# Recurrence scores of a gated linear mixer: 32-frame cells in 32-column matmuls in place of three 128-wide levels

## Chip, core and metric

One core of one Trainium2 chip runs the whole kernel in a single launch. The metric is the time of the device in microseconds, and the kernel before was timed three times: 842.62, 845.66 and 846.02 us, median 845.66 us.

## What is computed

The reference is one layer of an encoder over 512 frames of 1024 channels: RMSNorm, one wide input projection, a gMLP branch, an HGRN2 gated linear recurrence of 8 heads, sigmoid merge gates, an output projection, and a squared-ReLU MLP, all in fp32. The change touches only the recurrence. For one head, with q, k, f and v of 128 channels each:

```
S_t = diag(f_t) S_{t-1} + k_t v_t^T          o_t = S_t^T q_t
# evaluated by chunks; inside a chunk
scores[t, s] = sum_d q[t, d] * k[s, d] * prod_{s < u <= t} f[u, d]     for s <= t, else 0
o_intra = scores @ v
```

The product of gates between s and t differs in every channel, so a score is a matmul only after the decays have been multiplied into the queries and the keys. The kernels do so by levels of distance between s and t.

## The kernel before, in words

A fp32 weight or activation is split into a high and a low part of a faster fp32 format (`split`, L93 to L95: ScalarE writes H, VectorE writes L), and a product is three matmuls (`mm3`, L118 to L120). Weights come in tiles of 128x1024 by DMA (`raw`, 4 buffers) and are split into `WH` and `WL` (5 buffers each).

The recurrence runs in four rounds of two heads. `proj_round` projects values V (`tok_proj`), then F, K and Q of each head (`chan_proj`), channels on partitions and the 512 frames (4 tiles of 128) on the free axis. `hgrn_head` makes the scores of one head. The tile framework orders the instructions of each engine by its own estimate of the times, so the matmuls of a head stand between projection matmuls of later rounds, or of the output gate ZO after the last one. [...]

In `hgrn_head`:

- The diagonal: q*k (L412, VectorE), split (L415, L416), two 512-wide matmuls with a matrix of ones (`dg`, L418, L419), and a predicated copy of 512 columns into `scores` (L420).
- Three levels with b = 1, 4, 16 frames in a block. Each holds the queries of 4 blocks in a group, times the decays to 6 pairs of blocks (`QX`, L436, L438), and multiplies them with all 128 keys of the tile: four matmuls of 128 columns by 192 moving columns a level (`sp`, L443). Where key and query form one of the pairs, a predicated copy takes the value into `scores` (L452, three copies for each half of the frames). Then queries and keys are moved on to the next level by more decay (L468 to L479).
- The level of 64 frames: four matmuls of 64 by 64 in half of TensorE's columns (L485), copied by ScalarE (L487), then K and Q moved on (L490 to L496).
- K turned onto frames (`pk`, L500), tile states (`pst`, L505; `st`, L507 to L511), the output (`po`, L515, L517) and its norm (L519 to L523).

Every fp32 matmul is recorded as two weight loads and two matmuls: the 96 matmuls of L443 in the program stand as 192 in the trace.

Of the kernel before, what the change touches and what calls it, by code (L numbers as in the profile page):

```python
# [8 lines left out]
F32 = mybir.dt.float32  # L9
F32R = mybir.dt.float32r  # L10
I32 = mybir.dt.int32
AF = mybir.ActivationFunctionType
ALU = mybir.AluOpType
AX = mybir.AxisListType

P = 128
S = 512
D = 1024
NT = S // P
# [11 lines left out]

RADIX = [1, 4, 16]
PAIRS = [(1, 1), (2, 1), (3, 1), (2, 2), (3, 2), (3, 3)]


# [34 lines left out]
def trunk_kernel(ctx: ExitStack, tc: tile.TileContext, A: dict, out: bass.AP):  # L72
    nc = tc.nc
# [4 lines left out]
    wp = ctx.enter_context(tc.tile_pool(name="wp", bufs=1))  # L78
# [110 lines left out]
    ident = cst.tile([P, P], F32, name="ident")  # L189
# [153 lines left out]
    for t in range(NT):  # L343
        stt6 = gp.tile([P, 6], F32, tag="bn6", bufs=2, name="bn6")
        nc.vector.bn_stats(stt6, v[:, t, :])
        mv = gp.tile([P, 2], F32, tag="mv", bufs=2, name="mv")
# [5 lines left out]
    for g in range(NG):  # L352
# [6 lines left out]
        m = gp.tile([P, NT, P], F32, tag="m", bufs=2, name="m")  # L359
# [8 lines left out]
    hg = left2.enter_context(tc.tile_pool(name="hg", bufs=1, side="left", reuse_waits="tile"))  # L368
    ps_sc = left2.enter_context(tc.tile_pool(name="ps_sc", bufs=1, space=bass.MemoryType.PSUM))
    nc.sync.dma_start(hng, A["hg_norm_g"].rearrange("o v -> v o"))  # L370
    mask = []
    for lv, b in enumerate(RADIX):
        m = hg.tile([P, 384], I32, name=f"mask{b}")
        nc.sync.dma_start(m, A[f"mask{b}"])
        mask.append(m)
    diag = hg.tile([P, P], I32, name="diag")
    nc.sync.dma_start(diag, A["diag"])
    all_ones = hg.tile([P, P], F32R, name="all_ones")
    nc.vector.tensor_scalar(all_ones, ident, 0.0, 1.0, ALU.mult, ALU.add)
    scores = [hg.tile([P, NT, P], F32, name=f"scores{i}") for i in range(2)]  # L380
    for sc in scores:
        nc.gpsimd.memset(sc, 0.0)


    def proj_round(r):
# [7 lines left out]
        for h in (2 * r, 2 * r + 1):  # L393
# [5 lines left out]
            zq = chan_proj(ZQ + 128 * h)  # L399
            Q = hg.tile([P, S], F32, tag="Q1", bufs=2, name=f"Q1_{h}")  # L400
            sq = hg.tile([P, S], F32, tag="sq", bufs=2, name=f"sq{h}")
# [4 lines left out]

    def hgrn_head(V, h, F, K, Q):
        hc = slice((h % 2) * P, (h % 2 + 1) * P)
        sc = scores[h % 2]

        qk = wp.tile([P, S], F32, tag="S", bufs=2, name=f"qk{h}")
        nc.vector.tensor_tensor(qk, Q, K, ALU.mult)  # L412
        qkH = hg.tile([P, S], F32R, tag="qkH", bufs=2, name=f"qkH{h}")
        qkL = hg.tile([P, S], F32R, tag="qkL", bufs=2, name=f"qkL{h}")
        nc.scalar.activation(qkH, qk, AF.Copy)  # L415
        nc.vector.tensor_tensor(qkL, qk, qkH.bitcast(F32), ALU.subtract)  # L416
        dg = ps_sc.tile([P, S], F32, tag="sp", bufs=4, name=f"dg{h}")
        nc.tensor.matmul(dg, all_ones, qkH, start=True, stop=False)  # L418
        nc.tensor.matmul(dg, all_ones, qkL, start=False, stop=True)  # L419
        nc.vector.copy_predicated(sc, diag[:, None, :].broadcast_to([P, NT, P]),  # L420
                                  dg.rearrange("p (t c) -> p t c", c=P))
        QX = hg.tile([P, 7 * S // 4], F32, tag="QX", bufs=4, name=f"QX1_{h}").rearrange("p (g x b) -> p g x b", x=7, b=1)
        nc.vector.tensor_tensor(QX[:, :, 0:4, 0], Q.rearrange("p (g i) -> p g i", i=4),
                                F.rearrange("p (g i) -> p g i", i=4), ALU.mult)

        T = F
        for lv, b in enumerate(RADIX):
            G, g = S // (4 * b), P // (4 * b)  # L430
            T4 = T[:, :4 * G].rearrange("p (g i) -> p g i", i=4)

            def bc(t, n=G, b=b):
                return t[:, :, None].broadcast_to([P, n, b])

            nc.vector.tensor_tensor(QX[:, :, 4:6, :], QX[:, :, 2:4, :],  # L436
                                    T4[:, :, 1:3, None].broadcast_to([P, G, 2, b]), ALU.mult)
            nc.vector.tensor_tensor(QX[:, :, 6, :], QX[:, :, 5, :], bc(T4[:, :, 1]), ALU.mult)  # L438
            for t0 in range(0, NT, 2):
                sp = ps_sc.tile([P, S], F32, tag="sp", bufs=4, name=f"sp{h}_{b}_{t0}")  # L440
                for j in range(2):
                    t = t0 + j
                    nc.tensor.matmul(  # L443
                        sp[:, j * 192:(j + 1) * 192].rearrange("p (g c) -> p g c", g=g),
                        K[:, t * P:(t + 1) * P],
                        QX[:, t * g:(t + 1) * g, 1:7, :].rearrange("p g x b -> p g (x b)"),
                        start=True, stop=True)
                spv = sp[:, :384].rearrange("p (g x b) -> p g x b", x=6, b=b)
                mv = mask[lv].rearrange("p (g x b) -> p g x b", x=6, b=b)
                scv = sc[:, t0:t0 + 2, :].rearrange("p t (g i b) -> p (t g) i b", i=4, b=b)  # L450
                for x0, n, i0 in [(0, 3, 1), (3, 2, 2), (5, 1, 3)]:
                    nc.vector.copy_predicated(scv[:, :, i0:i0 + n, :], mv[:, :, x0:x0 + n, :],  # L452
                                              spv[:, :, x0:x0 + n, :])

            b4 = 4 * b
            if b < 16:
                QN = hg.tile([P, 7 * S // 4], F32, tag="QX", bufs=4, name=f"QX{b4}_{h}").rearrange("p (g x b) -> p g x b", x=7, b=b4)
                qn = QN[:, :, 0:4, :].rearrange("p g i (j b) -> p g i j b", b=b)
                n4 = 4
            else:  # L460
                QN = hg.tile([P, S], F32, tag="Q64", bufs=2, name=f"Q64_{h}")
                qn = QN.rearrange("p (g i j b) -> p g i j b", i=1, j=4, b=b)
                n4 = 1

            def grp(x, n4=n4):
                return x.rearrange("p (g i) b -> p g i b", i=n4)

            nc.scalar.copy(qn[:, :, :, 0, :], grp(QX[:, :, 0, :]))  # L468
            for j, x in ((1, 1), (2, 4), (3, 6)):
                nc.vector.tensor_tensor(qn[:, :, :, j, :], grp(QX[:, :, x, :]), grp(bc(T4[:, :, 0])), ALU.mult)  # L470
            U = hg.tile([P, G, 2], F32, tag=f"U{b}", bufs=2, name=f"U{b}_{h}")
            Tn = hg.tile([P, G], F32, tag=f"T{b}", bufs=2, name=f"T{b}_{h}")
            nc.vector.tensor_tensor(U[:, :, 1], T4[:, :, 2], T4[:, :, 3], ALU.mult)
            nc.vector.tensor_tensor(U[:, :, 0], T4[:, :, 1], U[:, :, 1], ALU.mult)
            nc.vector.tensor_tensor(Tn, T4[:, :, 0], U[:, :, 0], ALU.mult)
            kv = K.rearrange("p (g i b) -> p g i b", i=4, b=b)
            nc.vector.tensor_tensor(kv[:, :, 0:2, :], kv[:, :, 0:2, :],
                                    U[:, :, :, None].broadcast_to([P, G, 2, b]), ALU.mult)
            nc.vector.tensor_tensor(kv[:, :, 2, :], kv[:, :, 2, :], bc(T4[:, :, 3]), ALU.mult)  # L479
            QX, T = QN, Tn  # L480

        Q = QX
        sp = ps_sc.tile([P, 512], F32, tag="sp", bufs=4, name=f"sp{h}_64")
        for t in range(NT):
            nc.tensor.matmul(sp[0:64, t * 64:(t + 1) * 64], K[:, t * P:t * P + 64],  # L485
                             Q[:, t * P + 64:(t + 1) * P], start=True, stop=True)
        nc.scalar.copy(sc[0:64, :, 64:128], sp[0:64, 0:256].rearrange("p (t c) -> p t c", c=64))  # L487
        T2 = T.rearrange("p (t i) -> p t i", i=2)
        qv = Q.rearrange("p (t i b) -> p t i b", i=2, b=64)
        kv = K.rearrange("p (t i b) -> p t i b", i=2, b=64)  # L490
        Tt = hg.tile([P, NT], F32, tag="Tt", bufs=2, name=f"Tt_{h}")
        nc.vector.tensor_tensor(kv[:, :, 0, :], kv[:, :, 0, :],
                                T2[:, :, 1:2].broadcast_to([P, NT, 64]), ALU.mult)
        nc.vector.tensor_tensor(qv[:, :, 1, :], qv[:, :, 1, :],
                                T2[:, :, 0:1].broadcast_to([P, NT, 64]), ALU.mult)
        nc.vector.tensor_tensor(Tt, T2[:, :, 0], T2[:, :, 1], ALU.mult)  # L496

        pk = ps.tile([P, NT, P], F32, tag="hm", bufs=2, name=f"pk{h}")
        for t in range(NT - 1):
# [14 lines left out]
        for t in range(NT):  # L514
            nc.tensor.matmul(po[:, t, :], sc[:, t, :], V[:, t, hc], start=True, stop=t == 0)  # L515
            if t:
                nc.tensor.matmul(po[:, t, :], Q[:, t * P:(t + 1) * P], st[:, t - 1, :],  # L517
                                 start=False, stop=True)
# [139 lines left out]
    for f in range(NPLAIN, NF, 2):  # L658
        g = acts[f // 8][:, f % 8:f % 8 + 2, :]
# [26 lines left out]
    for t in range(NT):  # L686
        for hf in range(2):
            for f in range(NSLOW - 2, NSLOW):
                ff2(f, t, hf)
            c = x2[:, t, hf * S:(hf + 1) * S]  # L690
# [151 lines left out]
def _mask(b):  # L842

    import numpy as np

    s = np.arange(P)
    m = np.zeros((P, 2, P // (4 * b), len(PAIRS), b), np.int32)
    for g in range(P // (4 * b)):
        for x, (i, d) in enumerate(PAIRS):
            m[:, :, g, x, :] = (s // b == 4 * g + i - d)[:, None, None]  # L850
    return m.reshape(P, -1)


# [35 lines left out]
```

## Time and profile before

| | us |
|---|---|
| median of three runs | 845.66 |
| the profiled execution | 845.11 |
| its span, first to last instruction | 843.3 |
| TensorE (PE) busy | 826.8 |
| VectorE (DVE) busy | 637.1 |
| ScalarE (ACT) busy | 401.7 |

The recurrence occupies TensorE, between projections, from about 98 to 283 us. PE's weight loads (PEld) are shown apart from its matmuls, and consecutive matmuls overlap in the records, so the distance from start to start is what one costs, not its own duration.

### The profile page before, as it was taken

What the parts mean: (1) busy time and instruction counts of PE and PEld (TensorE: products, weight loads), DVE (VectorE), ACT (ScalarE), POOL (GpSimd) and SP (SyncE); (2) the same over time, 40 slices, a digit from 0 to 9 for tenths busy, and PEclk for the clock granted to TensorE, in tenths of its full rate; (3) what the DMA queues carried; (4) which work ended last, traced back from release to release, by engine and by line L of the source; (5) the groups of instructions that cost most, each with busy time, mean ns of one, the idle gap of its engine ahead of it and who ended that gap; (6) DMA issues with size and microseconds to landing.
All of it is one profiled execution on the core that took longest, in us unless ns stands there. A gap on an engine that the chain in (4) does not pass through costs nothing.

```text
span 843.3 us, 13369 instructions
## 1 busy us (share of the span) xinstructions
PE 826.8 (98%) x5282; PEld 745.7 (88%) x5282; DVE 637.1 (76%) x1092; ACT 401.7 (48%) x644; POOL 47.6 (6%) x79
## 2 busy tenths in 40 slices
PE   8999999999999999999999999899999999999996
PEld 7989898989889997999978889899999988778884
DVE  6563888979799587888565349877777574899996
ACT  6433433333242345656533332777766642555464
POOL 2000000001001000000000012000000000010103
PEclk9999999999999999999999999999999999999999
DMA  9233212121221121233423412132332295193802
GB/s 334 87 117 115 100 51 75 44 83 51 75 76 51 51 76 57 74 120 108 147 103 120 167 63 96 67 109 101 119 108 101 100 293 183 27 301 85 242 17 99
DMA packets 26912, 92.68 MB, mean 110 GB/s; under 512 B 3361, under 2 KB 3873, under 8 KB 26850
## 3 DMA queue, kind: packets, MB, share of 16 engines
q1 hardware_dynamic: 24546, 84.49, 28.2%
q0 software_dynamic: 1728, 6.29, 4.2%
q10 hardware_dynamic: 576, 1.05, 0.3%
q8 instruction: 41, 0.67, 0.3%
q14 instruction: 21, 0.17, 0.1%
HBM read 89.72 MB, written 2.10 MB: 109 GB/s over the span
## 4 chain that ended last, share of the span: by engine, by line
PE 94%; ACT 2%; issue 1%; DVE 1%; DMA 1%; POOL 0%; SPq 0%; POOLq 0%; ACTq 0%; DVEq 0%
PE acc L118 14%; PE acc L119 14%; PE acc L120 14%; PE prodx L118 5%; PE prodx L120 5%; PE prodx L119 5%; PE sp L443 4%; PE prodzy L119 4%; PE prodzy L118 4%; PE prodzy L120 4%; PE hm L119 3%; PE hm L120 3%; PE hm L118 3%; PE y L119 2%; PE y L118 2%; PE y L120 2%
## 5 line engine op out<-in xcount | busy, mean ns | idle before, releaser
L95 DVE TENSOR_TENSOR WL<-raw,WH 128x1024 fp32r<-128x1024 f32 (+1 forms) x134 | 152.1, 1138 | 100.3 <-ACT WH L94 99.3
L94 ACT ACTIVATE WH<-raw 128x1024 fp32r<-128x1024 f32 (+1 forms) x134 | 132.3, 989 | 182.0 <-PE acc L119 68.3
L118 PE MATMUL acc<-WH,hTH 128*128 128x256 f32 x320 | 91.7, 287 | 0.2 <-ACT hTH L94 0.2
L120 PE MATMUL acc<-WH,hTL 128*128 128x256 f32 x320 | 91.6, 286 | 0.0
L119 PE MATMUL acc<-WL,hTH 128*128 128x256 f32 x320 | 90.6, 283 | 0.0
L120 PE MATMUL acc<-hTH,WL 128*128 128x512 f32 x160 | 64.3, 402 | 0.0
L119 PE MATMUL acc<-hTL,WH 128*128 128x512 f32 x160 | 64.1, 401 | 0.0
L118 PE MATMUL acc<-hTH,WH 128*128 128x512 f32 x160 | 64.1, 400 | 0.0
L95 DVE TENSOR_TENSOR WL<-s,WH 128x1024 fp32r<-128x1024 f32 x44 | 53.8, 1223 | 9.8 <-ACT WH L94 9.0
L118 PEld LDWEIGHTS acc<-WH,hTH 128*128 128x128 f32 x320 | 60.4, 189 | 0.4 <-ACT hTH L94 0.4
L120 PEld LDWEIGHTS acc<-WH,hTL 128*128 128x128 f32 x320 | 60.3, 189 | 0.1
L119 PEld LDWEIGHTS acc<-WL,hTH 128*128 128x128 f32 x320 | 60.3, 189 | 0.0
L94 ACT ACTIVATE WH<-s 128x1024 fp32r<-128x1024 f32 x44 | 46.7, 1062 | 14.6 <-PE prodx L119 9.5
L452 DVE COPY_PREDICATED scores<-mask,sp 128x192 f32<-128x192 int32 (+2 forms) x144 | 44.1, 360 | 6.8 <-PE sp L443 6.4
L119 PE MATMUL hm<-WL,aH 128*128 128x512 f32 x96 | 38.1, 397 | 0.0
L120 PE MATMUL hm<-WH,aL 128*128 128x512 f32 x96 | 38.0, 396 | 0.0
L118 PE MATMUL hm<-WH,aH 128*128 128x512 f32 x96 | 37.9, 396 | 0.0
L443 PE MATMUL sp<-QX,K 128*128 128x192 f32 x192 | 35.9, 326 | 0.0
L120 PEld LDWEIGHTS acc<-hTH,WL 128*128 128x128 f32 x160 | 30.1, 188 | 6.4
L119 PEld LDWEIGHTS acc<-hTL,WH 128*128 128x128 f32 x160 | 30.1, 188 | 6.4
L118 PEld LDWEIGHTS acc<-hTH,WH 128*128 128x128 f32 x160 | 30.1, 188 | 6.2
L94 ACT ACTIVATE WH<-rawx 128x1024 fp32r<-128x1024 f32 x24 | 25.1, 1053 | 18.5 <-issue 10.7
(298 smaller groups left out, 2408.2 us busy)
## 6 DMA issues: line engine op xcount, KB each, us to landing
raw<-in_w_dram SPq DMA_DIRECT2D x128, 512.0 KB, 3.5
rawx<-in_w_dram SPq DMA_DIRECT2D x18, 512.0 KB, 8.1
rawx<-in_w_dram POOLq DMA_DIRECT2D x6, 512.0 KB, 6.4
raw<-in_w_dram POOLq DMA_DIRECT2D x6, 512.0 KB, 8.0
x_t<-in_x_dram SPq DMA_DIRECT2D x4, 512.0 KB, 5.9
x<-in_x_dram SPq DMA_DIRECT2D x4, 512.0 KB, 5.6
out_dram<-x ACTq DMA_DIRECT2D x4, 256.0 KB, 2.8
out_dram<-x SPq DMA_DIRECT2D x4, 256.0 KB, 2.4
```

Source lines behind the costliest of these rows:

```text
L94: nc.scalar.activation(H, src, AF.Copy)
L95: nc.vector.tensor_tensor(L, src, H.bitcast(F32), ALU.subtract)
L118: nc.tensor.matmul(acc, ah, bh, start=first and i == 0, stop=False, **kw)
L119: nc.tensor.matmul(acc, ah, bl, start=False, stop=False, **kw)
L120: nc.tensor.matmul(acc, al, bh, start=False, stop=last and i == n - 1, **kw)
L443: nc.tensor.matmul(sp[:, j * 192:(j + 1) * 192].rearrange("p (g c) -> p g c", g=g), K[:, t * P:(t + 1) * P], QX[:, t * g:(t + 1) * g, 1:7, ...
L452: nc.vector.copy_predicated(scv[:, :, i0:i0 + n, :], mv[:, :, x0:x0 + n, :], spv[:, :, x0:x0 + n, :])
```

## The change

The scores of a tile are no longer made 128 keys wide. A tile of 128 frames is cut into four cells of 32 frames (`C = 32`, `NC = 4`). Up to blocks of 16, key and query lie in one cell, so a matmul takes 32 keys as stationary columns and the queries of the same cell only, and writes to the 32 output partitions of that cell: its own quarter of TensorE's columns. The result of a level is compact: all four tiles of a head fit in one bank, and one set of predicated copies takes it into `cells`.

- Diagonal: q times k as 16 matmuls of 32 by 32; product, split, ones matmuls and the 512-wide copy are gone.
- Levels 1 and 4: 16 matmuls of 32 keys by 48 moving columns, in place of 4 of 128 by 192. The predicated copies stand behind the updates of K and Q in the code, three a level in place of six.
- Level 16 is replaced by two halvings: blocks of 16 (16 matmuls of 32 by 16) and blocks of 32 (8 matmuls of 32 by 32), each followed by an in-place update of K and Q (`double`).
- ScalarE moves the four cells and the two 32-frame blocks into `scores` (six copies of 32 partitions).
- Level 64 is as before (L512 in the changed kernel).

```diff
-RADIX = [1, 4, 16]
+RADIX = [1, 4]
+C = 32
+NC = P // C
...
-        qk = wp.tile([P, S], F32, tag="S", bufs=2, name=f"qk{h}")
-        nc.vector.tensor_tensor(qk, Q, K, ALU.mult)
...
-        nc.scalar.activation(qkH, qk, AF.Copy)
-        nc.vector.tensor_tensor(qkL, qk, qkH.bitcast(F32), ALU.subtract)
-        dg = ps_sc.tile([P, S], F32, tag="sp", bufs=4, name=f"dg{h}")
-        nc.tensor.matmul(dg, all_ones, qkH, start=True, stop=False)
-        nc.tensor.matmul(dg, all_ones, qkL, start=False, stop=True)
-        nc.vector.copy_predicated(sc, diag[:, None, :].broadcast_to([P, NT, P]),
-                                  dg.rearrange("p (t c) -> p t c", c=P))
+        def cellwise(sp, x, n, of=1):
+            for t in range(NT):
+                for p in range(0, NC, of):
+                    nc.tensor.matmul(sp[p * C:(p + 1) * C, t * n:(t + 1) * n],
+                                     K[:, t * P + p * C:t * P + (p + 1) * C], x(t, p), start=True, stop=True)
...
+        sp = bank(0)
+        cellwise(sp, lambda t, p: Q[:, t * P + p * C:t * P + (p + 1) * C], C)
+        nc.vector.copy_predicated(cl.rearrange("p t c -> p (t c)"), mask[0], sp[:, :NT * C])
...
-            for t0 in range(0, NT, 2):
-                sp = ps_sc.tile([P, S], F32, tag="sp", bufs=4, name=f"sp{h}_{b}_{t0}")
-                for j in range(2):
-                    t = t0 + j
-                    nc.tensor.matmul(
-                        sp[:, j * 192:(j + 1) * 192].rearrange("p (g c) -> p g c", g=g),
-                        K[:, t * P:(t + 1) * P],
-                        QX[:, t * g:(t + 1) * g, 1:7, :].rearrange("p g x b -> p g (x b)"),
-                        start=True, stop=True)
...
-                for x0, n, i0 in [(0, 3, 1), (3, 2, 2), (5, 1, 3)]:
-                    nc.vector.copy_predicated(scv[:, :, i0:i0 + n, :], mv[:, :, x0:x0 + n, :],
-                                              spv[:, :, x0:x0 + n, :])
+            sp = bank(b)
+            cellwise(sp, lambda t, p: QX[:, (t * NC + p) * g:(t * NC + p + 1) * g, 1:7, :].rearrange(
+                "p g x b -> p g (x b)"), 6 * g * b)
...
+            for x0, n, i0 in [(0, 3, 1), (3, 2, 2), (5, 1, 3)]:
+                nc.vector.copy_predicated(clv[:, :, i0:i0 + n, :], mv[:, :, x0:x0 + n, :],
+                                          spv[:, :, x0:x0 + n, :])
...
+        def double(T, b):
+            n = S // (2 * b)
+            T2 = T.rearrange("p (g i) -> p g i", i=2)
+            Tn = hg.tile([P, n], F32, tag=f"T{b}", bufs=2, name=f"T{b}_{h}")
+            nc.vector.tensor_tensor(Tn, T2[:, :, 0], T2[:, :, 1], ALU.mult)
+            qv = Q.rearrange("p (g i b) -> p g i b", i=2, b=b)
+            kv = K.rearrange("p (g i b) -> p g i b", i=2, b=b)
+            nc.vector.tensor_tensor(kv[:, :, 0, :], kv[:, :, 0, :], T2[:, :, 1:2].broadcast_to([P, n, b]), ALU.mult)
+            nc.vector.tensor_tensor(qv[:, :, 1, :], qv[:, :, 1, :], T2[:, :, 0:1].broadcast_to([P, n, b]), ALU.mult)
+            return Tn
...
+        sp = bank(16)
+        cellwise(sp, lambda t, p: Q[:, t * P + p * C + 16:t * P + (p + 1) * C], 16)
+        T = double(T, 16)
+        nc.vector.copy_predicated(cl[:, :, 16:32], mask[3].rearrange("p (t c) -> p t c", t=NT),
+                                  sp[:, :NT * 16].rearrange("p (t c) -> p t c", t=NT))
+        for p in range(NC):
+            nc.scalar.copy(sc[p * C:(p + 1) * C, :, p * C:(p + 1) * C], cl[p * C:(p + 1) * C])
+        sp = bank(32)
+        cellwise(sp, lambda t, p: Q[:, t * P + (p + 1) * C:t * P + (p + 2) * C], C, 2)
+        for p in range(0, NC, 2):
+            nc.scalar.copy(sc[p * C:(p + 1) * C, :, (p + 1) * C:(p + 2) * C],
+                           sp[p * C:(p + 1) * C, :NT * C].rearrange("p (t c) -> p t c", t=NT))
+        T = double(T, C)
```

What this makes of TensorE's order is seen where head 0 ends and head 1 begins. A row is line, operation, output from inputs, the moving operand's shape and a count; `sp1_4` is head 1, level 4 (before, a third number is the first of two tiles), and the last number only tells allocations apart. Before:

```order
L119 MATMUL acc_1343<-hTL_82,WH_1339 128x512
L485 MATMUL sp0_64_1042<-Q64_0_1030,K0_844 64x64 x4
L418 MATMUL dg1_1094<-qkH1_1090,all_ones_693 128x512
L419 MATMUL dg1_1094<-qkL1_1091,all_ones_693 128x512
L443 MATMUL sp1_1_0_1102<-QX1_1_1098,K1_914 128x192 x2
L443 MATMUL sp1_1_2_1108<-QX1_1_1098,K1_914 128x192 x2
L120 MATMUL acc_1343<-hTH_81,WL_1340 128x512
```

The same place in the changed kernel, whose lines are four or more higher (L122 to L124 are `mm3`, L417 is `cellwise`):

```order
L123 MATMUL acc_1423<-hTL_82,WH_1419 128x512
L512 MATMUL sp0_64_1083<-Q16_0_1027,K0_846 64x64 x4
L417 MATMUL sp1_0_1129<-Q1_1_950,K1_916 32x32 x16
L417 MATMUL sp1_1_1151<-QX1_1_1146,K1_916 32x48 x16
L124 MATMUL acc_1423<-hTH_81,WL_1420 128x512
L519 MATMUL pk0_1093<-ident_64,K0_846 128x128 x3
```

Six matmuls of full width between the 64-frame group and the projection have become 32 matmuls of a quarter of the columns.

The second place is level 4 of head 1, again on TensorE, in the changed kernel:

```order
L123 MATMUL acc_1458<-hTL_82,WH_1454 128x512
L417 MATMUL sp1_4_1185<-QX4_1_1168,K1_916 32x48
L524 MATMUL pst0_1099<-V0_701,kd0_1097 128x128 x3
L534 MATMUL po0_1107<-V0_701,scores0_693 128x128
L417 MATMUL sp1_4_1185<-QX4_1_1168,K1_916 32x48 x15
L124 MATMUL acc_1458<-hTH_81,WL_1455 128x512
```

Before, the four matmuls of this level (L443) stood in one piece between projection matmuls; now the sixteen stand in two pieces, with four full-width matmuls of head 0 between them. Over the whole program the matmuls that use only some of the columns stand in 8 unbroken groups before, and in 53 now; in six places a group of 64 columns and one of 32 follow each other with no full-width matmul between.

## Rows read from the trace of the kernel before

**Rows 1.** The page: busy time by engine; the chain that ended last, by engine.

```profile
PE 826.8 (98%) x5282; PEld 745.7 (88%) x5282; DVE 637.1 (76%) x1092; ACT 401.7 (48%) x644; POOL 47.6 (6%) x79
...
PE 94%; ACT 2%; issue 1%; DVE 1%; DMA 1%; POOL 0%; SPq 0%; POOLq 0%; ACTq 0%; DVEq 0%
```

**Rows 2.** Busy time by stretch: window, length, engines (x instructions), PE clock, DMA.

```profile
98.00:283.00 185.00, 185.00 (x1210) 168.46 (x1209) 160.08 (x496) 63.68 (x150) 10.25 (x13) 1.00 0.18 64
```

**Rows 3.** Who PE waited for in the whole span: total us, times, longest.

```profile
PE prodx L118 <- ACT WH L94: 2.7, 2, 1.7
PE warm L293 <- POOL ident masks.py:199: 1.9, 1, 1.9
PE pt L284 <- DVE hTL L95: 0.9, 1, 0.9
...
```

**Rows 4.** Timeline of PE from 99.83 us, start, duration: the diagonal and level 1.

```profile
99.83 0.40 PE L418 MATMUL dg<-qkH,all_ones 128*128 128x512 f32 x1
100.07 0.39 PE L419 MATMUL dg<-qkL,all_ones 128*128 128x512 f32 x1
100.30 1.46 PE L443 MATMUL sp<-QX,K 128*128 128x192 f32 x8
```

**Rows 5.** The tile sp: weight loads and matmuls, min/median/max ns, first and last start.

```profile
L443 PE MATMUL sp<-QX,K x192: 323/326/328, 100.3 to 277.7; 128*128 128x192 f32 x192
L485 PEld LDWEIGHTS sp<-Q,K x64: 132/138/138, 117.5 to 282.2; 128*64 128x64 f32 x64
```

**Rows 6.** Timelines of PEld, then PE, around a 64-column group at 117.1 us.

```profile
117.51 0.54 PEld L485 LDWEIGHTS sp<-Q,K 128*64 128x64 f32 x8 [0.36 <-issue]
...
117.19 0.39 PE L119 MATMUL acc<-hTL,WH 128*128 128x512 f32 x1
117.51 0.68 PE L485 MATMUL sp<-Q,K 128*64 128x64 f32 x8
118.12 0.50 PE L418 MATMUL dg<-qkH,all_ones 128*128 128x512 f32 x1
118.46 0.40 PE L419 MATMUL dg<-qkL,all_ones 128*128 128x512 f32 x1
```

**Rows 7.** Timeline of PE around another such group, at 163.3 us.

```profile
163.58 0.28 PE L120 MATMUL acc<-WH,hTL 128*128 128x256 f32 x1
163.79 0.68 PE L485 MATMUL sp<-Q,K 128*64 128x64 f32 x8
164.40 0.50 PE L418 MATMUL dg<-qkH,all_ones 128*128 128x512 f32 x1
164.74 0.39 PE L419 MATMUL dg<-qkL,all_ones 128*128 128x512 f32 x1
```

**Rows 8.** Timeline at 421.05 us, PE empty and released by VectorE.

```profile
421.07 0.20 PEld L562 LDWEIGHTS py<-ident,o_n 128*128 128x128 f32 x2 [0.84 <-issue]
421.10 0.30 PE L562 MATMUL py<-ident,o_n 128*128 128x128 f32 x1 [0.43 <-DVE ybL L565]
```

**Rows 9.** VectorE's groups from 98 to 283 us: busy us, mean ns, idle before.

```profile
L452 DVE COPY_PREDICATED scores<-mask,sp 128x192 f32<-128x192 int32 x48 | 18.1, 399 | 6.4 <-PE sp L443 6.4
L452 DVE COPY_PREDICATED scores<-mask,sp 128x64 f32<-128x64 int32 x48 | 14.0, 323 | 0.2
L420 DVE COPY_PREDICATED scores<-diag,dg 128x512 f32<-128x512 int32 x8 | 5.9, 737 | 0.4 <-PE dg L419 0.4
L492 DVE TENSOR_TENSOR K<-K,T 128x256 f32<-128x256 f32 x8 | 3.4, 419 | 0.2 <-PE sp L485 0.2
```

**Rows 10.** ScalarE's groups in the same stretch.

```profile
L94 ACT ACTIVATE WH<-raw 128x1024 fp32r<-128x1024 f32 x22 | 23.3, 1060 | 35.1 <-PE acc L119 24.0 <-PE acc L120 11.1
L487 ACT COPY scores<-sp 64x256 f32<-64x256 f32 x8 | 2.9, 365 | 4.6 <-PE sp L485 4.6
```

**Rows 11.** Busy time by stretch around PE's longest wait; columns as in rows 2.

```profile
531.00:535.80 4.80, 2.89 (x23) 2.48 (x21) 4.80 (x7) 4.80 (x8) 0.00 (x0) 1.00 0.22 75
535.80:539.20 3.40, 2.83 (x13) 2.83 (x14) 2.39 (x3) 1.91 (x6) 0.00 (x0) 0.50 0.13 51
```

More of the change, by code (lines that the diff above doesn't have):

```diff
@@ L371, in trunk_kernel @@
     mask = []
-    for lv, b in enumerate(RADIX):
-        m = hg.tile([P, 384], I32, name=f"mask{b}")
+    for b in (0, *RADIX, 16):
+        n = {0: C, 16: 16}.get(b, 6 * C // 4)
+        m = hg.tile([P, NT * n], I32, name=f"mask{b}")
         nc.sync.dma_start(m, A[f"mask{b}"])
         mask.append(m)
[L376 to L379, printed above, removed]
     scores = [hg.tile([P, NT, P], F32, name=f"scores{i}") for i in range(2)]
-    for sc in scores:
+    cells = [hg.tile([P, NT, C], F32, name=f"cells{i}") for i in range(2)]
+    for sc in (*scores, *cells):
         nc.gpsimd.memset(sc, 0.0)
@@ L408, in hgrn_head, with bank @@
         hc = slice((h % 2) * P, (h % 2 + 1) * P)
-        sc = scores[h % 2]
-        qk = wp.tile([P, S], F32, tag="S", bufs=2, name=f"qk{h}")
-        nc.vector.tensor_tensor(qk, Q, K, ALU.mult)
-        qkH = hg.tile([P, S], F32R, tag="qkH", bufs=2, name=f"qkH{h}")
-        qkL = hg.tile([P, S], F32R, tag="qkL", bufs=2, name=f"qkL{h}")
-        nc.scalar.activation(qkH, qk, AF.Copy)
-        nc.vector.tensor_tensor(qkL, qk, qkH.bitcast(F32), ALU.subtract)
-        dg = ps_sc.tile([P, S], F32, tag="sp", bufs=4, name=f"dg{h}")
-        nc.tensor.matmul(dg, all_ones, qkH, start=True, stop=False)
-        nc.tensor.matmul(dg, all_ones, qkL, start=False, stop=True)
-        nc.vector.copy_predicated(sc, diag[:, None, :].broadcast_to([P, NT, P]),
-                                  dg.rearrange("p (t c) -> p t c", c=P))
-        QX = hg.tile([P, 7 * S // 4], F32, tag="QX", bufs=4, name=f"QX1_{h}").rearrange("p (g x b) -> p g x b", x=7, b=1)
+        sc, cl = scores[h % 2], cells[h % 2]
+        def cellwise(sp, x, n, of=1):
[3 more added lines that the diff above has]
+                                     K[:, t * P + p * C:t * P + (p + 1) * C], x(t, p), start=True, stop=True)
+        def bank(name):
+            return ps_sc.tile([P, S], F32, tag="sp", bufs=4, name=f"sp{h}_{name}")
+        sp = bank(0)
+        cellwise(sp, lambda t, p: Q[:, t * P + p * C:t * P + (p + 1) * C], C)
+        QX = hg.tile([P, 7 * S // 4], F32, tag="QX", bufs=3, name=f"QX1_{h}").rearrange("p (g x b) -> p g x b", x=7, b=1)
         nc.vector.tensor_tensor(QX[:, :, 0:4, 0], Q.rearrange("p (g i) -> p g i", i=4),
                                 F.rearrange("p (g i) -> p g i", i=4), ALU.mult)
+        nc.vector.copy_predicated(cl.rearrange("p t c -> p (t c)"), mask[0], sp[:, :NT * C])
         T = F
         for lv, b in enumerate(RADIX):
-            G, g = S // (4 * b), P // (4 * b)
+            G, g = S // (4 * b), C // (4 * b)
             T4 = T[:, :4 * G].rearrange("p (g i) -> p g i", i=4)
@@ L438, in hgrn_head @@
             nc.vector.tensor_tensor(QX[:, :, 6, :], QX[:, :, 5, :], bc(T4[:, :, 1]), ALU.mult)
-            for t0 in range(0, NT, 2):
-                sp = ps_sc.tile([P, S], F32, tag="sp", bufs=4, name=f"sp{h}_{b}_{t0}")
-                for j in range(2):
-                    t = t0 + j
-                    nc.tensor.matmul(
-                        sp[:, j * 192:(j + 1) * 192].rearrange("p (g c) -> p g c", g=g),
-                        K[:, t * P:(t + 1) * P],
-                        QX[:, t * g:(t + 1) * g, 1:7, :].rearrange("p g x b -> p g (x b)"),
-                        start=True, stop=True)
-                spv = sp[:, :384].rearrange("p (g x b) -> p g x b", x=6, b=b)
-                mv = mask[lv].rearrange("p (g x b) -> p g x b", x=6, b=b)
-                scv = sc[:, t0:t0 + 2, :].rearrange("p t (g i b) -> p (t g) i b", i=4, b=b)
-                for x0, n, i0 in [(0, 3, 1), (3, 2, 2), (5, 1, 3)]:
-                    nc.vector.copy_predicated(scv[:, :, i0:i0 + n, :], mv[:, :, x0:x0 + n, :],
-                                              spv[:, :, x0:x0 + n, :])
+            sp = bank(b)
+            cellwise(sp, lambda t, p: QX[:, (t * NC + p) * g:(t * NC + p + 1) * g, 1:7, :].rearrange(
+                "p g x b -> p g (x b)"), 6 * g * b)
             b4 = 4 * b
-            if b < 16:
-                QN = hg.tile([P, 7 * S // 4], F32, tag="QX", bufs=4, name=f"QX{b4}_{h}").rearrange("p (g x b) -> p g x b", x=7, b=b4)
+            if lv == 0:
+                QN = hg.tile([P, 7 * S // 4], F32, tag="QX", bufs=3, name=f"QX{b4}_{h}").rearrange("p (g x b) -> p g x b", x=7, b=b4)
                 qn = QN[:, :, 0:4, :].rearrange("p g i (j b) -> p g i j b", b=b)
@@ L460, in hgrn_head @@
             else:
-                QN = hg.tile([P, S], F32, tag="Q64", bufs=2, name=f"Q64_{h}")
+                QN = hg.tile([P, S], F32, tag="Q16", bufs=2, name=f"Q16_{h}")
                 qn = QN.rearrange("p (g i j b) -> p g i j b", i=1, j=4, b=b)
@@ L479, in hgrn_head @@
             nc.vector.tensor_tensor(kv[:, :, 2, :], kv[:, :, 2, :], bc(T4[:, :, 3]), ALU.mult)
+            spv = sp[:, :NT * 48].rearrange("p (g x b) -> p g x b", x=6, b=b)
+            mv = mask[1 + lv].rearrange("p (g x b) -> p g x b", x=6, b=b)
+            clv = cl.rearrange("p t (g i b) -> p (t g) i b", i=4, b=b)
+            for x0, n, i0 in [(0, 3, 1), (3, 2, 2), (5, 1, 3)]:
+                nc.vector.copy_predicated(clv[:, :, i0:i0 + n, :], mv[:, :, x0:x0 + n, :],
+                                          spv[:, :, x0:x0 + n, :])
             QX, T = QN, Tn
         Q = QX
-        sp = ps_sc.tile([P, 512], F32, tag="sp", bufs=4, name=f"sp{h}_64")
+        def double(T, b):
[21 more added lines that the diff above has]
+        T = double(T, C)
+        sp = bank(64)
         for t in range(NT):
@@ L487, in hgrn_head @@
         nc.scalar.copy(sc[0:64, :, 64:128], sp[0:64, 0:256].rearrange("p (t c) -> p t c", c=64))
[L488 to L496, printed above, removed]
+        Tt = double(T, 64)
         pk = ps.tile([P, NT, P], F32, tag="hm", bufs=2, name=f"pk{h}")
@@ L844, in _mask @@
     import numpy as np
[L846 to L851, printed above, removed]
+    s = np.arange(P) % C
+    if b == 0:
+        m = (s[:, None] == np.arange(C)).astype(np.int32)
+    elif b == 16:
+        m = np.repeat((s < 16)[:, None], 16, axis=1).astype(np.int32)
+    else:
+        m = np.zeros((P, C // (4 * b), len(PAIRS), b), np.int32)
+        for g in range(C // (4 * b)):
+            for x, (i, d) in enumerate(PAIRS):
+                m[:, g, x, :] = (s // b == 4 * g + i - d)[:, None]
+    return np.tile(m.reshape(P, -1), (1, NT))
 def kernel(**inputs):
@@ L865 @@
         "wsT": i["gmlp_ws"][0].transpose(2, 0, 1),
-        "mask1": _mask(1),
-        "mask4": _mask(4),
-        "mask16": _mask(16),
-        "diag": _np.eye(P, dtype=_np.int32),
+        **{f"mask{b}": _mask(b) for b in (0, *RADIX, 16)},
         "gmlp_ln_g": i["gmlp_ln_g"][0],
```

## The prediction

> **What bounds the kernel now.** I read the page's busy times and chain first. TensorE is busy 98% of the span, and the chain that ended last runs through it for 94% [rows 1]. The busy times by stretch then show that in the stretch of the recurrence, 98 to 283 us, PE is busy for all of its 185.00 us, VectorE for 160.08, ScalarE for 63.68 [rows 2]. Last I read who PE waits for: the longest entries are waits of 2.7, 1.9 and 0.9 us in other stages, and no line of the recurrence stands in the list [rows 3]. So VectorE, though loaded to 87% there, is never what PE waits for, and the time changes by what the change does to PE's queue. What a matmul costs there is the distance from one start to the next. The sum is made against the profiled execution, 845.11 us, half a microsecond under the median of 845.66.
>
> **What goes, on PE.** Of a head, two matmuls with ones go; their starts lie 0.235 us apart [rows 4], together 0.47. Of L443, 24 recorded matmuls go: eight of them took 1.46 us with the last one's 0.326 in it, so (1.46 - 0.326) / 7 = 0.162 us each [rows 4, 5], together 3.89. With the eight of L485, which stay and cost 0.0574 each ((0.54 - 0.138) / 7, from the weight loads [rows 5, 6]), or 0.46, a head's scores cost 4.82 us. All of that is on the path, since PE never rests.
>
> **What comes, on PE.** Diagonal, level 1, level 4 and the halving at 16 are 16 matmuls each, the one at 32 is 8: with two records each, 32 + 32 + 32 + 32 + 16 = 144 pairs of a weight load and a matmul. No row shows a 32-column matmul, so I bound a pair.
>
> - By the array, if pairs run one after another: L443 shows 0.162 us for 192 moving columns, 0.84 ns a column. L485 needs 54 ns for its 64 by that rate and takes 57.4, so some 3.5 ns are added for each pair, and its weight load (64 columns) is hidden or no longer than that. A pair with 32 moving columns is then 27 + 3.5 = 30.5 ns, with 48 it is 44, and with 16 the weight load of 32 columns, half of L485's, keeps it at 30.5. A head: 0.98 + 1.41 + 1.41 + 0.98 + 0.49, and 0.46 for L512, is 5.72 us. That is 0.90 more than before: fewer columns are streamed for each key, but with only a quarter of the array at work.
> - From above: 57.4 ns a pair whatever its size, the shortest distance that any row shows. 144 of them and 0.46 are 8.73 us, 3.91 more.
> - From below: four quarters fully side by side, which is a rival below.
>
> Which end? L485 is the nearest row, and it runs at the array's pace. But a group there has 8 pairs; diagonal and level 1 now make one of 64, which is longer than anything the profile shows at short distances. What feeds the array can be read where PE stood empty and a wait of VectorE ended: a weight load at 421.07, its matmul at 421.10, the next weight load 58 ns after the first (two in 0.20 us, of 0.14 each) [rows 8]. So in the open a pair is handed over in at most 58 ns. For the group of 64 I take the middle of 2.39 (array) and 3.67 (57.4 a pair), 0.65 more, and the array's pace for the shorter ones. A head is 6.37 us, 1.55 more, and eight heads are **+12.4 us**.
>
> [...]
>
> **Entering and leaving.** A group of 64-column matmuls costs more than its pairs. From the last projection matmul before it (117.19) to the second matmul after it (118.46) are 1.27 us [rows 6]; two 512-wide distances (0.47) and eight pairs (0.46) explain 0.93, so 0.34 us are lost around one group: the first start comes late, and the first matmul after the group is followed late as well. Another group, between 256-wide and 512-wide matmuls, gives 164.74 - 163.58 = 1.16, less 0.12 (half a 512-wide), 0.235 and 0.46, again 0.34 [rows 7]. Before there are 8 groups. Now there are 53, and in six places 64 columns meet 32 without a full-width matmul between, so 47 are bounded by full-width matmuls. 39 more at 0.34 are 13.3 us; an inner change from 64 to 32 lies between 0 and 0.34, I take half: 1.0. Together **+14.3 us**.
>
> **VectorE and ScalarE, at nothing.** VectorE loses eighteen predicated copies of 0.32 to 0.40 us a head and one of 0.74 [rows 9], about 7.2 us, product and split of the diagonal, and level 16 of QX. It gains seven copies no wider than the 0.323 row (one is 128 wide) and four updates like L492's 0.42. Its load falls by some us a head, but what it gives back is idle time, since PE did not wait for it. ScalarE gains six copies near L487's 0.365 a head (2.2 us) and loses a split and one copy. The weight splits queued behind them, L94, themselves waited 35.1 us for PE to free their buffers [rows 10], so they lead by far more than those copies; if that lead were gone, a late WH would stall PE as at 535 us. The updates between the halvings (0.84 us for K and Q) lie under 12 or more projection matmuls, 1.4 us at 0.12 each; without that cover each would cost up to its 0.84. The mask loads stay four in number and are smaller.
>
> **Sum.** 845.1 + 12.4 + 14.3 = 871.8, so **872 us**.
>
> **The rivals.**
>
> *Quarters side by side (faster).* Consecutive matmuls go to different quarters. If four stream at once, the 5.26 us of the 144 pairs become 1.31, a head 1.77, and eight heads save 24.4 us; less 14.3 that is 835 us. It decides below 17.8 ns a pair: (4.82 - 0.46 - 14.3 / 8) / 144. For it: the four have separate columns and outputs. Against: rows 8 show 27 to 31 ns from load to matmul and from matmul to load, where PE was empty, so a long group would starve. If the weight loads are taken on beside the matmuls and only one step of about 27 ns a pair is left, a head is 4.35 and the time 845.1 - 3.8 + 14.3 = 856.
>
> [...]
>
> *Every pair pays 57 ns (slower still).* 3.91 x 8 = 31.3, and 14.3: 891 us. For it: no shorter distance stands in the trace. Against: L485's fits its columns.
>
> [...]
>
> *VectorE was the bound after all.* Then its lost load would shorten the stretch; PE's 185.00 busy of 185.00 speaks against it, and I give it no chance of its own.
>
> **How the numbers follow.** Pairs one after another, 856 to 884 us: 0.58. All pairs dear, or the clock falling, 884 to 900: 0.20. Quarters partly side by side, within 0.5% of the median (which is about what a measurement of this kernel can tell from no change): 0.08; a little above that, to 856: 0.04. Fully side by side: 0.10. So faster 0.10, same 0.08, slower 0.82. The range 848 to 898 leaves out the fast case, half of the even one, and the far end of the dear one.
>
> **What would show it.** In the changed profile, L417's matmuls should start 30 to 58 ns apart inside a group, 44 for level 1 and 4; starts 10 ns apart, or matmuls of different quarters that start together, would show the rival. The first full-width matmul after a group should come, and be followed, late as in rows 6. The recurrence should take some 27 us longer with PE busy throughout; VectorE's predicated copies should fall to about a third. A granted clock of 0.50 between 98 and 310 us, or waits of PE for VectorE at L417, would make the prediction wrong by another cause.

## The result and the profile after

The changed kernel takes 834.67 us, median of four runs (833.13 to 836.09), beside 844.38 us of the kernel before in the same comparison: ratio 0.9885, 95% interval 0.9855 to 0.9916. It is 1.15% faster. 872 us was forecast, with 848 as the lower end: wrong, and on the wrong side. The rival "quarters side by side" gave 835 us.

The page's busy times, by engine, of the changed kernel, which answer to [rows 1]:

```profile
PE 818.7 (98%) x6226; PEld 730.5 (88%) x6226; DVE 599.2 (72%) x955; ACT 408.5 (49%) x676; POOL 47.1 (6%) x81
```

TensorE has 944 recorded matmuls more and is busy for 8.1 us less. Busy time by stretch, as in [rows 2]:

```profile
98.00:283.00 185.00, 185.00 (x2233) 160.89 (x2232) 127.62 (x368) 73.42 (x187) 10.59 (x14) 1.00 0.22 69
```

PE still has no idle time there, at a granted clock of 1.00; VectorE's load in the same 185 us has gone from 160.08 to 127.62. So the bound is where the prediction put it, and no new wait came in. What differs is what a pair costs. The timeline of PE at the first group, to be held against [rows 4]:

```profile
99.46 0.46 PE L417 MATMUL sp<-Q,K 128*32 128x32 f32 x32
99.73 0.57 PE L417 MATMUL sp<-QX,K 128*32 128x48 f32 x32
100.23 0.39 PE L122 MATMUL acc<-WH,hTH 128*128 128x256 f32 x1
```

and the tile sp, durations of one matmul in ns, min/median/max:

```profile
L417 PE MATMUL sp<-Q,K x640: 182/196/217, 99.5 to 272.1; 128*32 128x32 f32 x96, 128*32 128x16 f32 x64
L417 PE MATMUL sp<-QX,K x512: 206/206/230, 99.7 to 263.7; 128*32 128x48 f32 x171
```

The 32 pairs of the diagonal start (0.46 - 0.196) / 31 = 8.5 ns apart, the 32 of level 1 (0.57 - 0.206) / 31 = 11.7 ns. The forecast had 30.5 and 44. Four times the measured distances are 34 and 47, near the forecast's pace of one quarter: the four quarters run at once. The weight loads do so too (PEld, same place):

```profile
99.46 0.35 PEld L417 LDWEIGHTS sp<-Q,K 128*32 128x32 f32 x32 [0.37 <-issue]
99.70 0.46 PEld L417 LDWEIGHTS sp<-QX,K 128*32 128x32 f32 x32
```

The timeline around level 4 of head 0 gives the price of a group again, as in [rows 6, 7]:

```profile
104.13 0.28 PE L124 MATMUL acc<-WH,hTL 128*128 128x256 f32 x1
104.33 0.55 PE L417 MATMUL sp<-QX,K 128*32 128x48 f32 x32
104.81 0.39 PE L122 MATMUL acc<-WH,hTH 128*128 128x256 f32 x1
105.03 0.28 PE L123 MATMUL acc<-WL,hTH 128*128 128x256 f32 x1
```

105.03 - 104.13 = 0.90, less two 256-wide distances (0.24) and 32 pairs at 11.1 ns (0.36), leaves 0.30 us lost around the group, where 0.34 was forecast.

The two halvings of head 0, blocks of 16 and of 32:

```profile
108.08 0.45 PE L417 MATMUL sp<-Q,K 128*32 128x16 f32 x32
111.84 0.45 PE L417 MATMUL sp<-Q,K 128*32 128x32 f32 x16
```

With 16 moving columns a pair costs 8.6 ns, (0.45 - 0.182) / 31, about as much as with 32. The 16 pairs of the blocks of 32 use only two quarters in turn and stand twice as far apart, (0.45 - 0.196) / 15 = 16.9 ns.

One thing outside the change moved. At the long wait that [rows 11] show, PE ran longer at the lower clock in this execution:

```profile
522.50:525.95 3.45, 1.70 (x15) 1.50 (x13) 3.45 (x5) 3.45 (x5) 0.00 (x0) 1.00 0.22 43
525.95:532.80 6.85, 6.21 (x29) 5.91 (x29) 4.77 (x6) 4.12 (x9) 0.00 (x0) 0.50 0.41 133
```

After a stretch in which PE was busy for 1.70 of 3.45 us, its granted clock was 0.50 for 6.85 us, in place of 3.40. Inside it 256-wide matmuls start 0.21 us apart, where they are 0.12 apart at 1.00 (timeline from 527.5 and from 532.8 us). By an estimate, half of the 3.45 us more, that takes up to 1.7 us from the difference of the profiled executions (836.09 against 845.11).

### The profile page after: what moved, and what is told of

Same layout as the page of the kernel before. It is cut to its first block, busy times and chain, and to the rows that moved or that the text cites. A ratio compares the mean times of both kernels' runs of the same rounds, so it can differ in the third digit from the quotient of the medians.

```text
span 834.2 us, 15111 instructions
## 1 busy us (share of the span) xinstructions
PE 818.7 (98%) x6226; PEld 730.5 (88%) x6226; DVE 599.2 (72%) x955; ACT 408.5 (49%) x676; POOL 47.1 (6%) x81
## 4 chain that ended last, share of the span: by engine, by line
PE 94%; DVE 2%; ACT 1%; issue 1%; POOL 1%; POOLq 0%; ACTq 0%; DVEq 0%
PE acc L122 15%; PE acc L124 15%; PE acc L123 15%; PE prodx L124 5%; PE prodx L122 5%; PE prodx L123 5%; PE prodzy L123 4%; PE prodzy L124 4%; PE prodzy L122 4%; PE hm L122 3%; PE hm L124 3%; PE hm L123 3%; PE y L122 2%; PE y L124 2%; PE y L123 2%; PE sp L417 2%
## 5 line engine op out<-in xcount | busy, mean ns | idle before, releaser
L122 PE MATMUL acc<-WH,hTH 128*128 128x256 f32 x320 | 91.5, 286 | 0.0
L124 PE MATMUL acc<-WH,hTL 128*128 128x256 f32 x320 | 91.3, 285 | 0.0
L122 PE MATMUL acc<-hTH,WH 128*128 128x512 f32 x160 | 64.2, 401 | 0.0
L124 PE MATMUL acc<-hTH,WL 128*128 128x512 f32 x160 | 64.2, 401 | 0.0
L122 PEld LDWEIGHTS acc<-WH,hTH 128*128 128x128 f32 x320 | 60.3, 189 | 0.6
L124 PEld LDWEIGHTS acc<-WH,hTL 128*128 128x128 f32 x320 | 60.3, 189 | 0.2
L124 PE MATMUL hm<-WH,aL 128*128 128x512 f32 x96 | 38.0, 395 | 0.0
L122 PE MATMUL hm<-WH,aH 128*128 128x512 f32 x96 | 37.9, 396 | 0.0
L124 PEld LDWEIGHTS acc<-hTH,WL 128*128 128x128 f32 x160 | 30.0, 188 | 7.1
L122 PEld LDWEIGHTS acc<-hTH,WH 128*128 128x128 f32 x160 | 30.0, 188 | 6.5
L122 PE MATMUL prodx<-h2H,WH 128*128 128x256 f32 x112 | 31.4, 280 | 1.8 <-ACT WH L98 1.8
L123 PE MATMUL prodzy<-h2L,WH 128*128 128x256 f32 x112 | 32.1, 287 | 0.0
```

The costliest lines, as they stand in the source:

```text
L122: nc.tensor.matmul(acc, ah, bh, start=first and i == 0, stop=False, **kw)
L123: nc.tensor.matmul(acc, ah, bl, start=False, stop=False, **kw)
L124: nc.tensor.matmul(acc, al, bh, start=False, stop=last and i == n - 1, **kw)
```

## The experiments

Two theories stand against each other, and two more had to be excluded. **Side by side**: matmuls in different quarters run at the same time, each at the array's pace. **Cheap anywhere**: a small matmul costs some 10 ns wherever it lies. **Hand-over**: a long group is limited by the 58 ns a pair read at 421 us, and the groups here are too short to show it. **VectorE**: its relief made the gain.

**Quarter outside, tile inside** (`quarter_major`). The same matmuls, but four of a quarter (eight pairs) in a row:

```diff
-            for t in range(NT):
-                for p in range(0, NC, of):
+            for p in range(0, NC, of):
+                for t in range(NT):
```

> The changed kernel with the loops of its cell matmuls exchanged: quarter outside, tile inside, so that four matmuls in a row use the same quarter of the columns; the work is the same. If quarters work side by side (theory), pairs on one quarter follow one another at 32 ns (32 or 16 columns) and 43 ns (48 columns): 80 x 32 + 64 x 43 = 5.3 us a head in place of 1.46, and with 43 groups between full-width matmuls in place of 47 the time is 834.7 + 30.8 - 1.3 = 864 us. If a small matmul is simply cheap wherever it lies (rival), the time stays at 833 to 835 us.

Measured: 851.51 us, ratio to the kernel before 1.009 (1.0058 to 1.0123). With nothing changed but the order inside a group, the gain is gone and more. "Cheap anywhere" falls. The size is off: 16.8 us more than the changed kernel where 29.5 were expected. The timeline of the first group says why:

```profile
99.54 0.80 PE L417 MATMUL sp<-Q,K 128*32 128x32 f32 x29
100.16 0.23 PE L417 MATMUL sp<-QX,K 128*32 128x48 f32 x1
100.18 0.23 PE L417 MATMUL sp<-Q,K 128*32 128x32 f32 x2
100.22 0.21 PE L417 MATMUL sp<-QX,K 128*32 128x48 f32 x1
100.25 0.20 PE L417 MATMUL sp<-Q,K 128*32 128x32 f32 x1
100.27 1.02 PE L417 MATMUL sp<-QX,K 128*32 128x48 f32 x30
101.21 0.39 PE L122 MATMUL acc<-WH,hTH 128*128 128x256 f32 x1
```

The group lasts from 99.54 to 101.21, 1.67 us in place of 0.77. The diagonal's pairs are (0.80 - 0.196) / 28 = 21.6 ns apart, neither 8 nor 32. And a matmul of level 1 (input QX) starts at 100.16, before the diagonal's last three (input Q) at 100.18 and 100.25, which stand ahead of it in the code. Each matmul has two records, so the odd counts, 29 and 1, can't come from whole matmuls queued in another order. The rows don't name the quarter, but the code does, and one reading fits both numbers: TensorE starts a matmul whose quarter is free before earlier ones that wait for theirs, so at each change of quarter two quarters overlap.

**Two quarters in turn** (`two_quarters`).

```diff
-            for t in range(NT):
-                for p in range(0, NC, of):
+            for half in range(0, NC, 2):
+                for t in range(NT):
+                    for p in range(half, half + 2, of):
```

> The same with pairs of quarters outside: matmuls in a row alternate between two quarters only, and the level of 32 frames uses one after the other. Side by side: two at a time, 64 / 2 x 32 + 64 / 2 x 43 + 16 x 32 ns = 2.9 us a head, 1.45 more, and 44 groups in place of 47: 834.7 + 11.6 - 1 = 845 us. Cheap anywhere: 833 to 835 us.

Measured: 841.13 us, ratio 0.9969 (0.995 to 0.9987): between the two orders, 6.5 us over the changed kernel where 10.6 were expected. The first group shows the same overlap at the changes:

```profile
99.88 0.51 PE L418 MATMUL sp<-Q,K 128*32 128x32 f32 x26
100.20 0.24 PE L418 MATMUL sp<-QX,K 128*32 128x48 f32 x2
100.22 0.23 PE L418 MATMUL sp<-Q,K 128*32 128x32 f32 x4
100.27 0.21 PE L418 MATMUL sp<-QX,K 128*32 128x48 f32 x2
100.28 0.20 PE L418 MATMUL sp<-Q,K 128*32 128x32 f32 x2
```

**Each quarter's matmuls twice before the next quarter** (`quarter_long`), to see how far ahead TensorE looks.

```diff
-            for t in range(NT):
-                for p in range(0, NC, of):
+            for p in range(0, NC, of):
+                for again in range(2):
+                    for t in range(NT):
```

> As the kernel with the quarter outside and the tile inside (851.5 us), but each quarter's matmuls are issued twice before the next quarter's turn, 16 pairs on one quarter in a row in place of 8. If matmuls of another quarter start ahead of those that wait for theirs only when they stand a few places behind, the added 144 pairs a head run mostly one after another: between 0.022 us a pair (the pace of the diagonal with 8 in a row) and 0.037, 25 to 42 us more, 877 to 894 us. If a quarter that is free is found however far behind its matmuls stand: four at a time, 11.7 us more, 863 us.

Measured: 896.12 us, ratio 1.0611 (1.0587 to 1.0634), 44.6 over `quarter_major`. It has 12 more groups; with 0.35 us for each, an estimate near the 0.30 above, the other 40.4 us are 35 ns for each of the 1152 added pairs. It is 2 us over the upper end given, which had left those 12 groups out. The first group:

```profile
99.94 1.82 PE L418 MATMUL sp<-Q,K 128*32 128x32 f32 x61
101.57 0.23 PE L418 MATMUL sp<-QX,K 128*32 128x48 f32 x1
101.60 0.23 PE L418 MATMUL sp<-Q,K 128*32 128x32 f32 x2
101.64 0.21 PE L418 MATMUL sp<-QX,K 128*32 128x48 f32 x1
101.66 0.20 PE L418 MATMUL sp<-Q,K 128*32 128x32 f32 x1
101.68 2.38 PE L418 MATMUL sp<-QX,K 128*32 128x48 f32 x62
```

The diagonal's pairs are (1.82 - 0.196) / 60 = 27.1 ns apart with 16 in a row, 21.6 with 8. So eight more pairs on a quarter add 16 x 27.1 - 8 x 21.6 = 261 ns, 33 each; for level 1 the same working gives 43. That is the pace of one quarter alone: the added pairs run one after another, and only what is saved at the change of quarter stays the same. The rows also show how far TensorE looks. Three diagonal pairs still wait when the first pair of level 1 starts, with 8 in a row (29 of 32 started) and with 16 (61 of 64); with two quarters in turn it is six (26 of 32), three for each quarter. In these orders a free quarter was found only that few places behind.

**Every group twice** (`twice`), the quarters in the changed kernel's order.

```diff
-            for t in range(NT):
-                for p in range(0, NC, of):
+            for again in range(2):
+                for t in range(NT):
+                    for p in range(0, NC, of):
```

> Every group of cell matmuls is issued a second time into the same place, so a group has up to 128 pairs in a row. Side by side, with the hand-over of instructions never short: 1.46 us a head more and 56 groups in place of 47, 834.7 + 11.7 + 3 = 849 us, and inside the group four starts in 32 or 43 ns as before. If instructions are handed over at the 58 ns a pair that the prediction took for the bound of long groups, and short groups only hide it: 144 x 0.058 x 8 = 67 us more, about 900 us.

Measured: 850.81 us, ratio 1.0077 (1.0053 to 1.0102). "Hand-over" falls: it gave about 900. The timeline of a group of 128 pairs:

```profile
100.26 0.73 PE L418 MATMUL sp<-Q,K 128*32 128x32 f32 x62
100.81 0.21 PE L418 MATMUL sp<-QX,K 128*32 128x48 f32 x1
100.81 0.20 PE L418 MATMUL sp<-Q,K 128*32 128x32 f32 x1
...
100.84 0.87 PE L418 MATMUL sp<-QX,K 128*32 128x48 f32 x62
101.64 0.38 PE L122 MATMUL acc<-WH,hTH 128*128 128x256 f32 x1
```

128 pairs in 101.64 - 100.26 = 1.38 us, 10.8 ns each with no gap at the end: instructions are handed over at least that fast.

**Work added to VectorE** (`vector_load`), seven times a head at five places:

```diff
+        def spare(n):
+            for _ in range(n):
+                nc.vector.tensor_tensor(spent, spent, spent, ALU.mult)
...
+            spare(2)
             QX, T = QN, Tn
```

> Seven multiplications of 512 columns on VectorE that nobody reads are added to each head, 7 x 0.70 x 8 = 39 us, as much as VectorE's busy time has fallen (637.1 to 599.2). If the gain is TensorE's alone: 834 to 836 us. If the relief of VectorE made the gain (rival): back to about 844 us.

Measured: 835.36 us, ratio 0.9892 (0.9859 to 0.9925). The multiplications took 39.1 us of VectorE:

```profile
L424 DVE TENSOR_TENSOR spent<-spent 128x512 f32<-128x512 f32 x56 | 39.1, 699 | 0.4
```

Its busy time in the whole span rose from 599.2 to 628.9 us, four fifths of the way back to 637.1, and the time did not follow: the kernel lies where "TensorE's alone" put it, 9 us under the rival. The relief is worth nothing here that these runs can tell from noise, as the prediction had it.

**The price of a group.** Two kernels carry the same three matmuls, which nobody reads, at each level 4: behind the group (`full_behind`), or between its tiles (`full_inside`).

```diff
+            def wide():
+                nc.tensor.matmul(sp[:, 384:512], ident, ident, start=True, stop=True)
...
+                if full and t < NT - 1:
+                    wide()
```

> Three full-width matmuls of 128 columns that nobody reads are added behind each group of level 4: 24 of them, 48 recorded pairs at 0.108 us, 5.2 us. As many groups between full-width matmuls as in the changed kernel (47): 834.7 + 5.2 = 840 us under every theory.

> The same 24 full-width matmuls, but put between the four tiles of level 4, so that its group is broken into four pieces: 67 groups in place of 47. If entering and leaving costs 0.33 us each time (theory): 6.6 us over the kernel with the same matmuls behind the group, 846.5 us. If the late starts around a group are only a matter of the records, or of what happened to stand there (rival): 840 us, as with the matmuls behind.

Measured: 838.52 us, ratio 0.9931 (0.9916 to 0.9946), and 845.97 us, ratio 1.0027 (1.0016 to 1.0038). The first is 1.5 us under its forecast; the comparison needs only that both hold the same matmuls. Breaking the groups 20 times more costs 7.45 us, 0.37 each. The timeline of the broken group:

```profile
104.58 0.29 PE L420 MATMUL sp<-QX,K 128*32 128x48 f32 x8
104.81 0.49 PE L416 MATMUL sp<-ident 128*128 128x128 f32 x2
105.22 0.29 PE L420 MATMUL sp<-QX,K 128*32 128x48 f32 x8
105.45 0.49 PE L416 MATMUL sp<-ident 128*128 128x128 f32 x2
```

One round takes 105.22 - 104.58 = 0.64 us; 8 pairs at 11 ns and two at 112 (the distance in the trace of `full_behind`) explain 0.31, and 0.33 are lost. The 39 groups that the change adds cost it some 13 us, more than the 9.7 it gains.

**Fewer groups, held in one piece.** `unbroken_64q` puts each group into the framework's critical section, which nothing else is scheduled into (diagonal and level 1 share one), and cuts level 64 into 32-column matmuls; `paired` lets one section serve both heads of a round.

```diff
+            with tc.tile_critical():
+                if lv == 0:
+                    cellwise(sd, lambda t, p: Q[:, t * P + p * C:t * P + (p + 1) * C], C)
+                cellwise(sp, ...)
```

> The changed kernel with each group of cell matmuls kept in one piece (diagonal and level 1 in one), and the level of 64 frames cut into 32-column matmuls over all four quarters, the odd tiles on the upper two. 38 groups in place of 47, 3.0 us less; no change from 64 to 32 columns left, about 1 us less; level 64 four at a time in place of one after another on half the columns, 0.23 us a head, 1.9 us less: 834.7 - 5.9 = 829 us if groups and quarters cost what the traces say. If the scheduler had broken the groups for a reason (waits of full-width matmuls that come due), the gain is lost again: 833 to 836 us.

> Both heads of a round go through their levels together, so that one group serves two heads, and the level of 64 frames is done in 32-column matmuls: 20 groups in place of 47, 27 x 0.33 = 8.9 us less, and about 1 us for the changes from 64 to 32 columns: 834.7 - 9.9 = 825 us. If TensorE now waits for VectorE, since the updates of two heads lie behind one another between two groups (rival): 830 us or more, with waits of PE at the cell matmuls.

Measured: 861.21 us, ratio 1.0196 (1.0176 to 1.0215), and 865.55 us, ratio 1.0252 (1.0236 to 1.0268). The groups are fewer and the time far longer: both forecasts missed. TensorE's waits of the first, from 98 to 300 us:

```profile
PE sp L417 <- issue: 7.2, 16, 0.6
PE sp L417 <- POOL rr_h L218: 3.3, 1, 3.3
PE sp L417 <- ACT scores L522: 2.8, 2, 2.4
PE sp L417 <- ACT hjunk L547: 2.7, 6, 0.5
```

The cell matmuls wait for GpSimd's `rr_h` and ScalarE's `hjunk`, which they don't read. So it is the holding that waits, by all appearance for whatever the other engines have in hand; in the changed kernel the same view has no row for this stretch. Busy time of the first by stretch, columns as in [rows 2]:

```profile
98.00:283.00 185.00, 164.05 (x2003) 137.68 (x2003) 113.28 (x333) 65.49 (x172) 9.39 (x12) 0.98 0.21 62
164.00:172.00 8.00, 4.97 (x121) 4.14 (x120) 4.52 (x9) 5.08 (x14) 1.29 (x2) 1.00 0.31 86
172.00:175.41 3.41, 3.41 (x8) 2.67 (x9) 2.77 (x10) 0.00 (x0) 0.00 (x0) 0.50 0.29 115
```

TensorE is idle for 21 us of the recurrence. After a stretch with 4.97 of 8.00 us busy its granted clock is 0.50 for 3.41 us: a falling clock, which the prediction gives a share of its chances, but here behind waits. The mean clock of the 185 us is 0.98; by an estimate, 185 x 0.02, that costs some 3.7 us more.

**The same without the holding.** `level64_quarters` changes level 64 alone; `paired_free_q` takes both heads of a round through their levels together, with the same level 64, and leaves the order to the scheduler. The first edit stands above the dots, the second below.

```diff
         for t in range(NT):
-            nc.tensor.matmul(sp[0:64, t * 64:(t + 1) * 64], K[:, t * P:t * P + 64],
-                             Q[:, t * P + 64:(t + 1) * P], start=True, stop=True)
+            for p in range(2):
+                q0 = (t % 2) * 64 + p * C
+                nc.tensor.matmul(sp[q0:q0 + C, t // 2 * 64:(t // 2 + 1) * 64], K[:, t * P + p * C:t * P + (p + 1) * C],
+                                 Q[:, t * P + 64:(t + 1) * P], start=True, stop=True)
...
+        both = [hgrn_head(V, *hd) for hd in heads]
+        for _ in range(5):
+            groups = [next(g) for g in both]
+            for group in groups:
+                group()
```

> The changed kernel with only its level of 64 frames changed: 16 matmuls of 32 columns over all four quarters in place of 4 of 64 columns, ScalarE's copy in two halves. No group is held together by force. 16 pairs of 64 moving columns, four at a time at 57 ns, are 0.23 us in place of 0.46, 1.9 us over eight heads; the six changes from 64 to 32 columns go, about 1 us; groups stay 47: 834.7 - 2.9 = 832 us. If the loss of the version in which groups were held in one piece came from this level and not from the holding: 850 us or more.

> Both heads of a round go through their levels together as before, but nothing holds a group in one piece, and the level of 64 frames is spread over the quarters: 40 groups in place of 47. 7 x 0.35 = 2.5 us and 2.9 us for the level of 64: 834.7 - 5.4 = 829 us, if the holding was what made TensorE wait. If the order by pairs of heads itself makes TensorE wait for VectorE: 840 us or more, with waits of PE between 98 and 283 us.

Measured: 832.49 us, ratio 0.9859 (0.9839 to 0.988), and 830.67 us, ratio 0.9835 (0.9814 to 0.9857). Both fall within 2 us of where the prices of a pair and a group put them, and the second is the fastest here, 1.65% under the kernel before. Its interval touches that of the changed kernel at the edge, so of its lead over that one only the direction is clear; the first one's lead isn't clear of noise. The holding, not the pairing, had cost the time.

## Why the prediction was wrong

- **What bounds the kernel**: right. PE has 185.00 of 185.00 us busy in the recurrence before and after, and four fifths of VectorE's relief, taken back, changed nothing. The chance of 0.20 for 884 to 900 us counts in a falling clock. No run shows the clock fall from quarter-width groups alone: from 98 to 283 us it is 1.00 in the changed kernel, in `quarter_major`, in `two_quarters` and in `twice`, and it is lower in `unbroken_64q` (0.98) and `paired` (0.96), where TensorE waits.
- **What goes, on PE**: 4.82 us a head, from rows, and nothing measured speaks against it.
- **What comes, on PE: "Which end?"** This step failed. The pace of one quarter was sized well: 30.5 and 44 ns a pair were worked out, and the runs with 8 and 16 in a row give 33 and 43. But the likeliest case let the pairs run "one after another", because the nearest row, L485, shows them so. Those eight pairs all lie in the same half of the columns; in such an order nothing else could be seen. With the quarters in turn four run at once: the diagonal 32 x 8.5 ns, level 1 at 11.7, level 4 at 11.1, and 0.27 us each for the halvings at 16 and at 32 (two quarters in turn), together some 1.54 us for the 144 pairs, where 5.26 stood (5.91 with the long group's addition). A head's scores take 2.0 us in place of 6.37: the term of +12.4 us is -22.6 by the trace.
- **The hand-over**: used wrongly. At 421 us the second weight load came 58 ns after the first [rows 8]. The prediction called it an upper bound, and then took it for what a long group needs. 128 pairs at 10.8 ns in `twice` show the hand-over to be at least five times as fast there. The row also held down the chance of the rival that came true.
- **Entering and leaving**: right. 0.34 us a group was forecast; the traces show 0.30 (level 4 of head 0) and 0.33 (a round of `full_inside`), the times of `full_inside` and `full_behind` 0.37.
- **VectorE and ScalarE, at nothing**: right. VectorE gains eight predicated copies a head, where the prediction counted seven; no term hangs on it.
- **The sum by what was measured**: 8 x (2.0 - 4.82) = -22.6 and 14.3 make -8.3, so 836.8 beside the profiled 836.09. That they meet so closely is in part luck: the profiled execution holds up to 1.7 us of lower clock that the sum leaves out.

Open is what sets how far ahead TensorE looks. The three orders fit three waiting pairs for each quarter; no run varies it by itself. What the third of a microsecond around a group is spent on is open as well.

## What to carry to other kernels

Pairs of 32-column matmuls cost about a quarter each where the quarters stood in turn in the order of issue: 8.5 ns, and 33 on one quarter alone. The same work with each quarter's matmuls in a row took 16.8 us longer. Against that, an unbroken group of part-width matmuls among full-width ones cost 0.30 to 0.37 us here, entering and leaving together, so count the unbroken groups in the scheduled order, not in the code. And a row on a resource used one way (eight pairs on one half) says nothing about using it in turn: where the nearest row can't show the effect, give the rival that needs it more than a tenth.

## What the runs showed of the hardware that was not expected

- Weight loads of different quarters overlap as the matmuls do: one lasts 0.11 us (106 to 113 ns), 32 of them 0.35, so (0.35 - 0.11) / 31, some 8 ns from one to the next.
- By the reading above, TensorE started a matmul whose quarter was free ahead of earlier ones (`quarter_major`: level 1 at 100.16 us, the diagonal's last at 100.18 and 100.25), past three waiting pairs of each busy quarter and no more in the orders run here (the diagonal: 27.1 ns a pair in runs of 16, 21.6 in runs of 8, 8.5 in turn).
